# Latent-only projections of the second layer as plain fp32 matmuls on unsplit weights

## The chip, the cores and the metric

The kernel runs on one core of a Trainium2 chip. The metric is the device time of one execution in microseconds, the median of several. Engines: PE (TensorE matmul, with PEld its weight loads), DVE (VectorE), ACT (ScalarE), POOL (GpSimd), SP (SyncE, which issues most DMAs).

## The reference

A two-layer hybrid backbone over 256 latent tokens of width 1024, with 256 context tokens as a prefix. Each layer modulates the tokens, projects them with one combined input matrix, runs four mixers (bidirectional RWKV-7, bidirectional Hyena, short gated convolution, grouped-query attention), merges their outputs through gates, projects, normalises, and runs a mixture of experts.

```python
for l in range(DEPTH):
    ctx_out = l < DEPTH - 1
    h = modulate(x, sh_a, sc_a)
    hc = modulate(ctx, sh_ac, sc_ac)
    pa, pb, pcv, pd, pg = jnp.split(h @ wl, splits, axis=-1)
    ...
    else:                                       # the second layer
        pa_c = hc @ wl[:, :OFF_HYENA]
        pd_c_kv = hc @ wl[:, OFF_ATTN + Q_W:OFF_GATE]
    ya_c, ya = rwkv_mixer(pa_c, pa, ...)
    yd_c, yd = attention_mixer(pd_c_kv, pd_c_q, pd, ...)
    yb = hyena_mixer(pb, ...)
    ycv = short_conv_mixer(pcv, sconv_w[l])
    y = merge_branches((ya, yb, ycv, yd), pg, w_branch[l], w_out[l])
    x = layer_norm(ALPHA * x + g_a * y, ln1_g[l], ln1_b[l])

def merge_branches(ys, gate_proj, w_branch, w_out):
    gates = jax.nn.sigmoid(gate_proj)...
    merged = gates[:, :, 0] * (ys[0] @ w_branch[0])
    for n in range(1, N_BRANCHES):
        merged = merged + gates[:, :, n] * (ys[n] @ w_branch[n])
    return merged @ w_out
```

In the second layer only the latents have an output, so the context enters there through the recurrence and through the attention's keys and values alone. The RWKV receptance (r) and its output gate (g), the attention queries, the Hyena branch, the short convolution and the merge gates read only the 256 latents.

## The kernel before

Tokens lie along the free axis: a layer's modulated input hT has 512 columns, 256 of context and then 256 of latents, and its 1024 channels are eight slices (k) of 128 partitions. Products that need full fp32 are made of three fp32r matmuls: each operand is split into a high part (an ACT copy that rounds, L326) and a low part (a DVE subtraction, L327), and `mm3` (L355 to L357) multiplies high by high, low by high and high by low into one accumulator. The input hT is kept split in tiles hA (high) and hB (low).

`proj` (L716) makes one block of 128 output channels. It takes a weight tile of 128x1024 out of the load ring (`win` and `load`, L711 and L367; one DMA of 1 MB on SP's queue brings two blocks' weights), splits it into one of two tiles cv (`wsplit`), and issues 8 `mm3` into an accumulator. A block takes 512 columns in layer 0 and where the context is needed, and 256 (n0 = 256) for the latent-only blocks of layer 1. The ring has two slots, named "ring".

Layer 1 runs `build_hT1` (transposes, layer norm, modulation), the attention's projections, `rwkv`, whose projections are r, k, v and the low-rank parts, then `hyena` and `sconv` through `block` (six blocks each), `recur` and `merge`. The recurrence is four pairs (`rwkv_pair`): each prepares its decays (PE L876, DVE L877 first), forms products, and inverts a triangular system; the loop L968 and L970 and the passes L990 to L1008 are that inverse, L1012 copies its result. `finish` (L816) normalises and gates the recurrence's output (L841, L844). `merge` (L1288) takes the branches in the order 2, 3, 1, 0. For each of 8 channel blocks it makes one gate block with `proj`, a tanh on ACT (L1323), the branch product (two `mm3` on a split w_branch and a split branch output) and one or two DVE operations (L1330 to L1333). Steps of the adaptive modulation's weight product (`ada_steps`, L394) are put between blocks by `pump`.

Each engine executes its own instructions in a fixed order that the scheduler writes at build time. It sets the order by readiness in its own model, by the source order, and by the buffers: a tile tag such as "R4" or "ring" can be given again only when its last reader is done. Gate blocks are ready early, so the scheduler uses them as fill between the small products of the recurrence.

Of the kernel before, what the change touches and what calls it, by code (L numbers as in the profile page):

```python
# [165 lines left out]
def backbone(ctx: ExitStack, tc: tile.TileContext, a: dict, out: bass.AP, dbg=None):  # L166
# [482 lines left out]
    def build_hT1(arrive, second, third, ups):  # L649

        A = [unit("R9"), unit("TZ")]
        XT = [unit(t).rearrange("p (k c) -> p k c", c=512) for t in ("R4", "R8")]
        hh, hl = big("hA"), big("hB")
# [13 lines left out]
        def modulate(tp, k2):  # L667
            ts_ = slice(tp * 256, tp * 256 + 256)
            q = (ops if k2 % 2 else rps)()
            for j in range(2):  # L670
                for i in range(2):
                    PE.transpose(q[:, (2 * j + i) * 128:(2 * j + i) * 128 + 128],
                                 lnx[2 * tp + i][:, (2 * k2 + j) * 128:(2 * k2 + j) * 128 + 128], ident)
            for j in range(2):
                k = 2 * k2 + j
                src = q[:, j * 256:j * 256 + 256]
                x, h, lo = XT[k // 4][:, k % 4, ts_], hh[k // 4][:, k % 4, ts_], hl[k // 4][:, k % 4, ts_]
                c1, c0 = m[:, tp, 1, k:k + 1], m[:, tp, 0, k:k + 1]
                go(ACT, lambda: ACT.activation(h, src, AF.Identity, scale=c1, bias=c0))
                if k2 % 2:  # L680
                    go(DVE, lambda: DVE.tensor_scalar(x, src, c1, c0, op0=OP.mult, op1=OP.add))
                else:
                    go(ACT, lambda: ACT.activation(x, src, AF.Identity, scale=c1, bias=c0))
                eng = POOL if j else DVE
                go(eng, lambda: eng.tensor_tensor(lo, x, h.bitcast(F32), op=OP.subtract))
# [21 lines left out]
        for k2 in range(4):  # L707
            modulate(1, k2)
        return hh, hl

# [5 lines left out]
    def proj(src, hT, n0, cuts=()):  # L716

        hi, lo = early.pop(0) if early else wsplit(src)
        o = acc()[:, :512 - n0]
        for c0, c1 in zip((n0,) + cuts, cuts + (512,)):  # L720
            for k in range(8):
                mm3(o[:, c0 - n0:c1 - n0], (hi[:, k, :], lo[:, k, :]),
                    (hT[0][k // 4][:, k % 4, c0:c1], hT[1][k // 4][:, k % 4, c0:c1]), k == 0, k == 7)
        return o
# [31 lines left out]
    def rwkv(l, hT, ctx_out):  # L756
# [29 lines left out]
        w = win(l, 2)  # L786
        vTu = unit("R4")
        for b in range(2):
            t = vTu[:, b * 512:b * 512 + 512]
            mix(t, proj(w[:, :, 128 * b:128 * b + 128], hT, 0), l, 4 + b)  # L790
            q = rps()
# [24 lines left out]
        def finish():  # L816

            lb = unit("R4")[:, :256]
            POOL.dma_start(lb, rows_ap(a["rwkv_lnx_b"], l * 256, [[0, 128], [1, 256]]))
# [33 lines left out]
    def rwkv_pair(l, s, b, emit, kTb, rTb, V, Y, wad, wa, bon, N8):  # L853
# [4 lines left out]
        rot[0] += 1  # L858
        F = Cut(unit("R4"))
        kkr, kkd, at, lw = F(256), F(256), F(256), F(256)  # L860
# [329 lines left out]
    def attention(l, hT, ctx_out):  # L1190
        n0 = 0 if ctx_out else 256
        A, B = Cut(unit("R5")), Cut(unit("R6"))
        kt, qs = A(512), [A(512), A(512)]
# [94 lines left out]
    def merge(l, hT, n0, ys, order, finish):  # L1288
        W_ = 512 - n0
        if n0:  # L1290
            m0, WB = unit("R5"), unit("R6", F32R)
            mg = [m0[:, db * W_:db * W_ + W_] for db in range(8)]
        else:
            ms, WB = (unit("R5"), unit("R6")), unit("R8", F32R)
            mg = [ms[db // 4][:, (db % 4) * 512:(db % 4) * 512 + 512] for db in range(8)]
        for oi, n in enumerate(order):
            if oi == FIN[l]:
                ys[0] = finish()
            if oi == 3:
                rg["tags"], rg["n"] = ("ring", "ring", "R2", "R3"), 0  # L1300
                cvr["tags"], cvr["n"] = ("cv0", "cv1", "R4"), 0
            if oi == 3:
                mh, ml = [[unit(t, F32R).rearrange("p (k c) -> p k c", c=512) for t in ts]
                          for ts in (("R0", "R1"), ("R9", "TZ"))]
            pr = unit("R7", F32R)
            yh = pr[:, :1024].rearrange("p (b t) -> p b t", b=2)
            yl = pr[:, 1024:].rearrange("p (b t) -> p b t", b=2)
            split(ys[n][:, :, :W_], yh[:, :, :W_], yl[:, :, :W_])
            if oi == 0:
                raw = wt("y2", [128, 1024])  # L1310
            for db in range(8):
# [3 lines left out]
                if db % 2 == 0:  # L1315
                    wb = raw[:, db % 4 * 256:db % 4 * 256 + 512].rearrange("p (k c) -> p k c", k=2)
                    SP.dma_start(wb, rows_ap(a["w_branch"], (l * 4 + n) * C * D + db * 128,
                                             [[D, 128], [128 * D, 2], [1, 256]]))
                    wbs = WB[:, db % 4 * 512:db % 4 * 512 + 1024].rearrange("p (x k c) -> p x k c", x=2, k=2)
                    split(wb, wbs[:, 0], wbs[:, 1])  # L1320
                gp = proj(wg[:, :, (db % 2) * 128:(db % 2) * 128 + 128], hT, n0)
# [3 lines left out]
                cs = slice((db % 2) * 128, (db % 2) * 128 + 128)  # L1325
                for k in range(2):
                    mm3(q, (wbs[:, 0, k, cs], wbs[:, 1, k, cs]),
                        (yh[:, k, :W_], yl[:, k, :W_]), k == 0, k == 1)
# [407 lines left out]
    for l in range(DEPTH):  # L1736
# [44 lines left out]
        def block(i, wc=wc, l=l, hT=hT, n0=n0):  # L1781
# [3 lines left out]
            return proj(wc[i // 2][:, :, (i % 2) * 128:(i % 2) * 128 + 128], hT, n0)  # L1785

        ys[1] = hyena(l, block, n0, kf)
        ys[2] = sconv(l, lambda j: block(6 + j), n0)
# [165 lines left out]
```

## Time and profile before

| quantity | value |
|---|---|
| median of 3 runs | 1911.12 us (1905.01 to 1916.12) |
| profiled execution, device time | 1914.72 us |
| its span in the trace | 1912.9 us |
| mean granted clock, share of full | 0.934 |
| PE busy | 1679.5 us, 88% of the span |
| DVE busy | 884.5 us, 46% |
| ACT busy | 530.6 us, 28% |

Times of the trace below count from the start of the span. Layer 1's mixers lie from about 1100 to 1634 us. An instruction's duration on PE is that of a pipelined instruction, so the distance from start to start in an undisturbed row is its price, not the duration in its row. "Idle" time in a row stands with the instruction that came before its engine could go on, and PEclk is the granted clock as a share of full.

### The profile page before, as it was taken

How to read it: one execution, taken by the hardware profiler on the slowest of the kernel's cores; microseconds unless marked ns; L12 is line 12 of the kernel's file. 1: busy time of each engine (PE TensorE's matmuls, PEld its weight loads, DVE VectorE, ACT ScalarE, POOL GpSimd, SP SyncE). 2: the span in 40 equal slices, each digit the busy share in tenths (PEclk: the TensorE clock that was granted, in tenths of full speed). 3: DMA queues.
4: the chain of work that ended last, by engine and by line, in shares of the span. 5: the costliest groups of instructions: out<-in, count | busy, mean ns of one | idle time of the engine just before them, and what ended most of it. 6: DMA issues, size and time to landing. Idle time of an engine off the chain costs nothing. (4 is left out here: it accounts for less than half of the span.)

```text
span 1912.9 us, 24847 instructions
## 1 busy us (share of the span) xinstructions
PE 1679.5 (88%) x9683; PEld 1109.7 (58%) x9683; DVE 884.5 (46%) x1920; ACT 530.6 (28%) x935; POOL 223.4 (12%) x263
## 2 busy tenths in 40 slices
PE   4799999999999987999999919989889996999982
PEld 1467666766778875444444306767778895444430
DVE  4364458778554565101010076585887676200003
ACT  2253233433223311111011044543443352111101
POOL 4200121011000031000000041021120002000001
PEclk7899999999999995999999959988899997999996
DMA  9513553111243255883979953265212357879994
GB/s 367 212 40 131 183 188 111 50 62 51 76 138 116 101 196 191 287 337 117 378 273 375 403 196 129 82 224 192 67 62 86 117 180 289 337 281 420 420 421 163
DMA packets 123350, 384.82 MB, mean 201 GB/s; under 512 B 8791, under 2 KB 75103, under 8 KB 92383
## 3 DMA queue, kind: packets, MB, share of 16 engines
q1 hardware_dynamic: 106176, 329.41, 46.0%
q10 hardware_dynamic: 10238, 33.23, 4.7%
q0 software_dynamic: 6816, 20.58, 3.0%
q8 instruction: 77, 1.26, 0.3%
q14 instruction: 43, 0.34, 0.1%
HBM read 361.62 MB, written 21.56 MB: 200 GB/s over the span
## 5 line engine op out<-in xcount | busy, mean ns | idle before, releaser
L357 PE MATMUL acc<-hB,cv 128*128 128x512 f32 (+1 forms) x864 | 309.4, 359 | 9.9 <-POOL hB L616 9.8
L355 PE MATMUL acc<-hA,cv 128*128 128x512 f32 (+1 forms) x864 | 309.2, 358 | 7.1 <-ACT hA L610 3.9
L356 PE MATMUL acc<-hA,cv 128*128 128x512 f32 (+1 forms) x864 | 308.1, 357 | 4.2 <-DVE cv L327 4.2
L355 PEld LDWEIGHTS acc<-hA,cv 128*128 128x128 f32 x864 | 166.2, 192 | 44.6 <-issue 10.1
L357 PEld LDWEIGHTS acc<-hB,cv 128*128 128x128 f32 x864 | 165.8, 192 | 44.5 <-issue 12.8
L356 PEld LDWEIGHTS acc<-hA,cv 128*128 128x128 f32 x864 | 166.1, 192 | 34.4 <-issue 8.4
L327 DVE TENSOR_TENSOR cv<-ring,cv 128x1024 fp32r<-128x1024 f32 (+1 forms) x108 | 128.6, 1197 | 41.9 <-ACT cv L326 39.6
L1415 DVE TENSOR_TENSOR y<-XS,k 128x512 f32<-128x512 f32 x15 | 15.4, 1029 | 266.4 <-PE k L1403 265.7
L326 ACT ACTIVATE cv<-ring 128x1024 fp32r<-128x1024 f32 (+1 forms) x108 | 109.1, 1019 | 27.7 <-DMA ring<-in_w_in_dram 22.4
L1403 PE MATMUL k<-R,R 128*64 128x512 f32 (+1 forms) x288 | 108.5, 600 | 2.9 <-DMA R<-in_exp_w_dram 2.9
L394 PE MATMUL ada<-ring,csf 128*32 128x512 f32 x336 | 63.4, 665 | 13.3 <-ACT csf L230 10.1
L1403 PEld LDWEIGHTS k<-R,R 128*64 128x64 f32 (+1 forms) x288 | 36.6, 152 | 56.5 <-issue 50.8
L1323 ACT ACTIVATE gt<-acc 128x512 f32<-128x512 f32 (+1 forms) x64 | 31.3, 488 | 110.9 <-PE acc L357 102.7
L1403 PE MATMUL acc<-R,R 128*64 128x512 f32 (+1 forms) x160 | 60.3, 594 | 1.7 <-DMA R<-in_exp_w_dram 1.7
L1415 DVE TENSOR_TENSOR y<-XS,acc 128x512 f32<-128x512 f32 x7 | 7.2, 1028 | 114.4 <-PE acc L1403 114.4
L1332 DVE SCALAR_TENSOR_TENSOR gt<-gt,o 128x512 f32<-128x512 f32 (+1 forms) x48 | 26.5, 552 | 69.6 <-PE o L357 66.1
L1403 PE MATMUL k<-ring,R 128*64 128x512 f32 (+1 forms) x144 | 54.4, 609 | 0.0
L968 DVE TENSOR_TENSOR R<-R 128x32 f32<-128x32 f32 (+14 forms) x120 | 50.9, 424 | 1.7
L1535 DVE CAST m_ix<-o 128x1 int32<-128x1 f32 x14 | 2.2, 159 | 106.2 <-PE o L1533 106.2
L355 PE MATMUL o<-R,R 128*128 128x512 f32 (+1 forms) x128 | 45.7, 358 | 2.9 <-DVE R L1330 2.9
L357 PE MATMUL o<-R,R 128*128 128x512 f32 (+1 forms) x128 | 45.6, 358 | 1.1 <-DVE R L327 1.1
L1435 PE MATMUL k<-R,y 128*64 128x512 f32 (+1 forms) x124 | 45.6, 593 | 0.8 <-DVE y L1420 0.8
(565 smaller groups left out, 3386.7 us busy)
## 6 DMA issues: line engine op xcount, KB each, us to landing
R<-in_exp_w_dram SPq DMA_DIRECT2D x87, 1024.0 KB
ring<-in_w_in_dram SPq DMA_DIRECT2D x51, 1024.0 KB
ring<-in_ada_w_dram SPq DMA_DIRECT2D x42, 1024.0 KB
ring<-in_exp_w_dram SPq DMA_DIRECT2D x34, 1024.0 KB
cv<-in_exp_w_dram SPq DMA_DIRECT2D x31, 1024.0 KB
hB<-in_exp_w_dram SPq DMA_DIRECT2D x24, 1024.0 KB
TZ<-in_exp_w_dram SPq DMA_DIRECT2D x16, 1024.0 KB
y<-in_w_branch_dram SPq DMA_DIRECT2D x32, 256.0 KB
```

The source lines that it names most:

```text
L326: first = ACT.activation(hi, src, AF.Copy)
L327: DVE.tensor_tensor(lo, src, hi.bitcast(F32), op=OP.subtract)
L355: PE.matmul(o, lh, rh, start=start, stop=False)
L356: PE.matmul(o, ll, rh, start=False, stop=False)
L357: PE.matmul(o, lh, rl, start=False, stop=stop)
L394: PE.matmul(po[32 * q:32 * q + 32, :], csf[:, 2 * k:2 * k + 32], t[:, 512 * q:512 * q + 512], start=(k == 0), stop=(k == 7), skip_group_ch ...
L968: DVE.tensor_tensor(P4[:, :, :, :i + 1], T4[:, :, :, :i + 1], row[:, None, :, :].to_broadcast([128, 8, 2, i + 1]), op=OP.mult)
L1323: ACT.activation(gt, gp, AF.Tanh, scale=0.5)
L1332: DVE.scalar_tensor_tensor(gt, gt, 1.0, q, op0=OP.add, op1=OP.mult)
L1403: PE.matmul(q[c, :], t[:, k, c], w[x](k), start=(k == 0), stop=(k == 7), skip_group_check=n > 1)
L1415: DVE.tensor_tensor(t.rearrange("p (k c) -> p c k", k=4), act.rearrange("p (c k) -> p c k", k=4), p3.rearrange("p (c k) -> p c k", k=4), o ...
L1435: PE.matmul(p[h][c, :], t[:, k, c], w2[x](k)[:, h * 512:h * 512 + 512], start=(k == 0), stop=(k == 3), skip_group_check=n > 1)
```

## The change

In layer 1 alone, the blocks that read only latents are made of plain fp32 matmuls: `proj` issues 8 matmuls of 128x256 on the fp32 weights as they lie in the load tile and on the fp32 latents, without a split of the weights and without cv tiles. These are 47 blocks: g (1), r (2), Hyena (6), short convolution (6), gates (32). The two blocks of the attention queries, whose weight tile is given as 4-d, keep the split; so do the blocks of 512 columns, layer 0 and the output projection. For this `build_hT1` keeps the modulated latents in fp32 (one tile XT[1], in R4) and hands them out as hT[2]. The branch products of layer 1's `merge` become two plain matmuls per block; their weights are loaded into R7 and neither they nor the branch outputs are split.

R4 is taken by the latents now, so four users of it or of its successors move in layer 1: the v tile to R8, the tiles of `finish` and of the pairs to R6, the attention's second tile to TZ. The ring has more slots in layer 1: after the RWKV projections "ring", "ring", "cv0", "cv1", and two more for the last branch. The accumulator is taken ahead of the split in all blocks.

```diff
     def build_hT1(arrive, second, third, ups):
         A = [unit("R9"), unit("TZ")]
-        XT = [unit(t).rearrange("p (k c) -> p k c", c=512) for t in ("R4", "R8")]
+        XT = [unit(t).rearrange("p (k c) -> p k c", c=256) for t in ("R8", "R4")]
...
-                x, h, lo = XT[k // 4][:, k % 4, ts_], hh[k // 4][:, k % 4, ts_], hl[k // 4][:, k % 4, ts_]
+                x, h, lo = XT[tp][:, k, :], hh[k // 4][:, k % 4, ts_], hl[k // 4][:, k % 4, ts_]
...
-        return hh, hl
+        return hh, hl, XT[1]
...
     def proj(src, hT, n0, cuts=()):
+        o = acc()[:, :512 - n0]
+        if n0 and len(hT) == 3 and len(src.shape) == 3:
+            for k in range(8):
+                PE.matmul(o, src[:, k], hT[2][:, k, :], start=(k == 0), stop=(k == 7))
+            return o
         hi, lo = early.pop(0) if early else wsplit(src)
-        o = acc()[:, :512 - n0]
...
-        vTu = unit("R4")
+        vTu = unit("R8" if l else "R4")
...
-            lb = unit("R4")[:, :256]
+            lb = unit("R6" if l else "R4")[:, :256]
...
-        F = Cut(unit("R4"))
+        F = Cut(unit("R6" if l else "R4"))
...
-        A, B = Cut(unit("R5")), Cut(unit("R6"))
+        A, B = Cut(unit("R5")), Cut(unit("TZ" if l else "R6"))
...
     def merge(l, hT, n0, ys, order, finish):
         if n0:
-            m0, WB = unit("R5"), unit("R6", F32R)
+            m0, raw = unit("R5"), unit("R7")
...
-                rg["tags"], rg["n"] = ("ring", "ring", "R2", "R3"), 0
+                rg["tags"], rg["n"] = ("ring", "ring", "R2", "R3") + (("cv0", "cv1") if n0 else ()), 0
...
-            split(ys[n][:, :, :W_], yh[:, :, :W_], yl[:, :, :W_])
+            if not n0:
...
+                split(ys[n][:, :, :W_], yh[:, :, :W_], yl[:, :, :W_])
...
-                    split(wb, wbs[:, 0], wbs[:, 1])
+                    if not n0:
...
+                        split(wb, wbs[:, 0], wbs[:, 1])
...
                 for k in range(2):
+                    if n0:
+                        PE.matmul(q, wb[:, k, cs], ys[n][:, k, :W_], start=(k == 0), stop=(k == 1))
+                        continue
                     mm3(q, (wbs[:, 0, k, cs], wbs[:, 1, k, cs]),
                         (yh[:, k, :W_], yl[:, k, :W_]), k == 0, k == 1)
...
+        if l:
+            rg["tags"], rg["n"] = ("ring", "ring", "cv0", "cv1"), 0
         ys[1] = hyena(l, block, n0, kf)
         ys[2] = sconv(l, lambda j: block(6 + j), n0)
         recur()
```

The order on the engines moves with it. Line numbers of the changed kernel are 4 higher from `rwkv` on (L876 is L880 there) and 9 or 10 higher in the end of `merge`. The first rows are PE's before, at the first recurrence pair of layer 1. Names: acc is a block's accumulator, cv a split weight tile, k a small accumulator of the recurrence, ada that of the modulation.

```order
L355 MATMUL acc_7866<-hA_1140_6964,cv_1275_7863 128x256
L356 MATMUL acc_7866<-hA_1140_6964,cv_1275_7863 128x256
L357 MATMUL acc_7866<-hB_1142_6966,cv_1275_7863 128x256
L876 MATMUL k_8340<-R_1324_8337,cst 64x256 x2
L883 MATMUL k_8346<-R_1243_7538 128x256
L884 MATMUL k_8347<-R_1243_7538 128x256
L883 MATMUL k_8371<-R_1243_7538 128x256
L884 MATMUL k_8372<-R_1243_7538 128x256
L355 MATMUL acc_7922<-hA_1139_6963,cv_1281_7919 128x256
L355 MATMUL acc_7953<-hA_1139_6963,cv_1283_7950 128x256
L394 MATMUL ada_7199<-ring_7896,csf 32x512 x4
```

The same place on PE in the changed kernel, where R_1138 is the tile of fp32 latents and L721 the new matmul:

```order
L394 MATMUL ada_7852<-cv_1297_7969,csf 32x512 x4
L721 MATMUL acc_7985<-R_1138_6962,ring_7961 128x256 x2
L721 MATMUL acc_8021<-R_1138_6962,cv_1301_7996 128x256 x8
L394 MATMUL ada_7852<-ring_7998,csf 32x512 x4
L721 MATMUL acc_8035<-R_1138_6962,cv_1301_7996 128x256 x5
L394 MATMUL ada_7852<-ring_8004,csf 32x512 x4
L721 MATMUL acc_8035<-R_1138_6962,cv_1301_7996 128x256 x3
L880 MATMUL k_8055<-R_1309_8052,cst 64x256 x2
L887 MATMUL k_8061<-R_1243_7538 128x256
L888 MATMUL k_8062<-R_1243_7538 128x256
L887 MATMUL k_8086<-R_1243_7538 128x256
L888 MATMUL k_8087<-R_1243_7538 128x256
```

Before, acc_7866 is the second of the six Hyena blocks; the other four and the short convolution's six stand behind the recurrence's first products (acc_7922 and acc_7953 are the next two). In the changed kernel all twelve stand ahead of them, acc_8035 being the last.

The second place is DVE in the inverse loop of a recurrence pair, before (L1046, L1072 and L1077 are the other pair's work):

```order
L970 TENSOR_REDUCE R_1427_9038<-R_1427_9038 128x16
L1077 TENSOR_SCALAR Sf_9160<-sbd_92,ssc_8487 128x128
L968 TENSOR_TENSOR R_1427_9038<-R_1427_9038 128x16x5
L327 TENSOR_TENSOR cv_1617_10152<-ring_10109,cv_1617_10152 128x1024
L970 TENSOR_REDUCE R_1427_9038<-R_1427_9038 128x16
L1072 COPY Wn_9131<-k_9128 128x128
L968 TENSOR_TENSOR R_1427_9038<-R_1427_9038 128x16x6
L1046 COPY_PREDICATED am_86<-msk,k_9138 128x128
```

and in the changed kernel, in the same loop:

```order
L972 TENSOR_TENSOR R_1412_8753<-R_1412_8753 128x16x5
L1341 SCALAR_TENSOR_TENSOR gt_9808<-gt_9808,o_9810 128x256
L974 TENSOR_REDUCE R_1412_8753<-R_1412_8753 128x16
L1342 TENSOR_TENSOR R_1566_9575<-R_1566_9575,gt_9808 128x256
L972 TENSOR_TENSOR R_1412_8753<-R_1412_8753 128x16x6
L1076 COPY Wn_8846<-k_8843 128x128
L974 TENSOR_REDUCE R_1412_8753<-R_1412_8753 128x16
```

The split of the weights is gone from between the links of the loop. What still stands there is the gate arithmetic of `merge` and the other pair's work.

## Rows read from the trace of the kernel before

**Rows 1.** The page: busy time, share of the span and instructions of each engine.

```profile
PE 1679.5 (88%) x9683; PEld 1109.7 (58%) x9683; DVE 884.5 (46%) x1920; ACT 530.6 (28%) x935; POOL 223.4 (12%) x263
```

**Rows 2.** Timeline (start, length), and L1012 by its line, in layer 1.

```profile
1241.75 0.60 PE L793 MATMUL k<-cst,R 128*128 128x128 f32 x4
...
1248.57 0.41 DVE L877 TENSOR_SCALAR R<-k 128x256 f32<-128x256 f32 x1
...
L1012 DVE COPY TZ<-TZ x8: 269/288/291, 1331.3 to 1480.5; 64x256 f32<-64x256 f32 x8
...
1512.98 0.41 PE L844 MATMUL k<-cst,R 128*128 128x128 f32 x2 [1.05 <-DVE R L841]
```

**Rows 3.** Windows from first pair to finish, and tail; columns first.

```profile
core 0: us, PE busy (x) PEld busy (x) DVE busy (x) ACT busy (x) POOL busy (x), PEclk, DMA share, GB/s
1248.60:1331.30 82.70, 72.94 (x591) 53.34 (x587) 60.01 (x129) 34.58 (x65) 17.88 (x23) 0.88 0.59 202
1331.30:1383.90 52.60, 46.82 (x472) 40.50 (x470) 41.46 (x107) 23.19 (x47) 9.03 (x9) 0.90 0.26 85
1383.90:1435.40 51.50, 45.87 (x480) 39.52 (x475) 44.41 (x110) 24.41 (x50) 11.05 (x10) 0.93 0.20 66
1435.40:1480.20 44.80, 43.34 (x485) 38.68 (x485) 35.50 (x88) 16.71 (x31) 2.44 (x2) 1.00 0.27 86
1480.20:1512.40 32.20, 31.67 (x264) 29.16 (x260) 17.77 (x56) 10.27 (x22) 1.76 (x3) 1.00 0.14 43
sum 263.80, PE 240.64 PEld 201.20 DVE 199.14 ACT 109.16 POOL 42.16; mean PE 48.13 PEld 40.24 DVE 39.83 ACT 21.83 POOL 8.43
...
1513.00:1570.00 57.00, 54.98 (x451) 54.22 (x452) 42.48 (x75) 28.00 (x47) 0.38 (x1) 0.97 0.58 190
```

**Rows 4.** The same windows, DVE's splits of L327 alone (us, busy, count).

```profile
1248.60:1331.30 82.70, 14.67 (x12) 0.88 0.59 202
1331.30:1383.90 52.60, 8.29 (x9) 0.90 0.26 85
1383.90:1435.40 51.50, 8.71 (x8) 0.93 0.20 66
1435.40:1480.20 44.80, 6.24 (x6) 1.00 0.27 86
1480.20:1512.40 32.20, 3.13 (x3) 1.00 0.14 43
```

**Rows 5.** PE's waits from 1100 to 1600: us in total, times, longest.

```profile
PE acc L356 <- DVE cv L327: 4.2, 3, 2.8
...
PE acc L355 <- ACT cv L326: 2.2, 5, 0.8
```

**Rows 6.** Timeline of DVE in the inverse loop.

```profile
1397.86 0.30 DVE L968 TENSOR_TENSOR R<-R 128x80 f32<-128x80 f32 x1
1398.08 1.22 DVE L327 TENSOR_TENSOR cv<-ring,cv 128x1024 fp32r<-128x1024 f32 x1
1399.21 0.23 DVE L970 TENSOR_REDUCE R<-R 128x16 f32<-128x80 f32 x1
```

**Rows 7.** Timeline of PE at the end of the gates and the output projection.

```profile
1568.89 0.28 PE L357 MATMUL acc<-hB,cv 128*128 128x256 f32 x1
...
1569.95 0.28 PE L357 MATMUL acc<-hB,cv 128*128 128x256 f32 x1
...
1570.75 0.39 PE L355 MATMUL acc<-R,R 128*128 128x512 f32 x1
```

**Rows 8.** Plain fp32 matmuls, and a modulation step: timeline and one line's records.

```profile
227.03 3.19 PE L1157 MATMUL o<-cst,R 128*128 128x256 f32 x14
230.06 3.18 PE L1145 MATMUL o<-R,cst 128*128 128x256 f32 x14
...
1291.23 1.07 PE L394 MATMUL ada<-ring,csf 128*32 128x512 f32 x8
...
L1157 PE MATMUL o<-cst,R x48: 377/379/483, 224.6 to 1290.9; 128*128 128x256 f32 x48
```

## What I predict, before the changed kernel has run

> **What bounds the kernel now.** I read the page first: PE is busy for 88% of the span and DVE for 46% [rows 1]. That is a mean over stages, and the change touches only layer 1's mixers, so I cut that stretch by what ends its stages. The four passes of the recurrence end where the copies of L1012 and then the finish at L844 run [rows 2]. In a table by stage [rows 3] PE is busy for 240.6 of the 263.8 us from the first recurrence pair to the finish, and DVE for 199.1. Both are needed: the passes are a chain of small PE products and small DVE operations, and the gate blocks are fill between them. Where PE runs out of fill the granted clock falls (0.88 in the first stage, 0.90 and 0.93 in the next two, 1.00 later). The tail from the finish to the output projection is PE alone: 54.98 of 57 us. The splits stand in the DVE column of a second table [rows 4]: 41.0 us of L327 in the five stages. The waits show hardly any of that on PE: 4.2 and 2.2 us [rows 5]. They cost on DVE's own chain instead: a split of 1.22 us stands between two links of the inverse loop, L968 and L970, on an engine that runs in a written order [rows 6].
>
> **The price of a block.** The old block issues three fp32r matmuls of 128x256 per k-slice. In an undisturbed row of them the starts are (1569.95 - 1568.89) / 9 = 0.118 us apart [rows 7], so 0.353 us per k-slice. The new one issues one plain fp32 matmul on the same 256 columns. The trace before has such matmuls in the hyena transforms: L1157 and L1145, both with fp32 operands. The program issues L1157 24 times and the trace has 48 records, so each is two records; 14 records take 230.06 - 227.03 = 3.03 us [rows 8], 0.216 each, so 0.433 us per matmul. The change therefore adds 0.08 us of PE per k-slice. It makes 47 blocks of 8 and 32 branch products of 2, 440 matmuls: 440 x 0.433 = 190.5 against 1320 x 0.118 = 155.8, **+34.7 us of PE work**. Removed are 47 block splits, 1.2 us of DVE each [rows 6], the branch splits, and the ACT copy that goes ahead of each.
>
> **Where it lands, by the order of the changed program.** Up to the second transposes of V (L793, at 1241.75 [rows 2]) 85 fp32r matmuls (10.0 us) become 28 plain ones (12.1): +2.1. The relaid latents put some of the filter's DVE work ahead of the last step of the input transposition: 0 to 3 us, I take 0.4. V's second transposes then come at 1244.3.
>
> The largest step is one that the diff doesn't name. Before, PE's first recurrence product stands shortly behind V's transposes, and most hyena and short-convolution blocks are fill beside the first pass; DVE's L877 ran at 1248.57 [rows 2]. Now PE has all the hyena and short-convolution blocks ahead of it: 92 plain matmuls x 0.433 = 39.8; ten steps of the modulation of 1.07 us each [rows 8] = 10.7; the transforms, 16 plain matmuls = 6.9 and 0.5 of small ones. That is 57.9 us. I add 3.6 for waits: the transforms wait for POOL and ACT in a chain, and the weight tiles are now read straight from the load ring, so a slot is free only after its last matmul; the loads behind it in SP's queue wait, and so does PE. The loads there are 16 tiles of 1.05 MB in 61.5 us, 273 GB/s. The first stage moved 202 GB/s at a share of 0.59 [rows 3], which scales to 342, so 80%: I bound the ring at 0 to 6 us. First pair: 1244.3 + 61.5 = **1305.8 and a little, 1306, 57.5 us later** than before.
>
> In return the first pass runs without all that. Between L877 and the inverse DVE now has 95 instructions. Without its splits it had 60.0 - 14.7 = 45.3 us for 117 before, 0.39 each, so 37 us busy [rows 3, 4]. Idle time on top: at least the 14 us that DVE had in the last short stage (32.2 - 17.8), at most the 22.7 of the first one. 51 to 60 us; I take 56, nearer to the first stage, whose chain and low clock this is. That is 26.7 us less than 82.7. **First inverse: +31 us.**
>
> Passes two to finish took 181.1 us. On DVE 8.3 + 8.7 + 6.2 + 3.1 = 26.4 us of splits go [rows 4]; if all of it comes back, 155 us. PE's fill there hardly changes its price: 495 fp32r matmuls (58.4 us) make way for 134 plain ones (58.0), since part of the gates now stands ahead of the first inverse. So PE's own busy time, 167.7 us [rows 3], is the other bound, less some 4.5 us if the clock were full through the stretch; from there to the 176 that would be if only splits beside an idle PE came back. I take 167: **-14 us.** What is late next is PE's chain of small products, not the splits.
>
> The tail: 126 plain matmuls x 0.433 = 54.6 us and about 0.7 at its start, against 57.7 (1512.98 to 1570.75) [rows 2, 7]: -2.4. The first matmuls after it wait less for branch splits: -1.
>
> Edits at nothing: the moved buffers (R4 to R8 or R6, R6 to TZ), since no row shows a wait for these tags in layer 1; the earlier call of the accumulator; everything in layer 0, the output projection and the experts, whose instructions stand in the old order.
>
> **Sum.** 31 - 14 - 2.4 - 1 = +13.6, against the profiled execution of 1914.7 us: 1928.3. The median of the runs shown, 1911.1, is 0.2% below that execution, so on its terms 1924.7, **1925 us**. Bounds by the terms: first stage -5 to +4, the later passes -12 to +9, the ring -2 to +4, the filter -0.4 to +2.6; not all at once, so the forecast's own range is 1911 to 1939.
>
> **Rivals.**
>
> Rival A, the other side: PE takes the extra work into its gaps. From the first pair to the finish it idles 23.2 us, and at the clocks of the table some 9.9 + 5.3 + 3.6 = 18.8 us are lost to the lower level; with DVE freed of 41 us of splits PE could run through both. Then 263.8 - 42.0 + 34.7 = 256.5, -7.3, and with the tail -10.7: 1904, or 1900 on the median's terms. For it: the splits stand inside the inverse loop. Against it: the gaps lie where the chain waits, and the new order takes the fill away from the first pass, where 9.8 us of them and most of the lost clock are. It decides if PE idles under 8 us from the first pair to the finish, at a clock of 0.98 or more. The Trainium skill, "Perfetto Trace Analysis", section Identifying the Most-Contended Engine, says that busy matmul time is a poor measure of TensorE's headroom and that the weight loads' busy share should be read too. By that rule 201.2 of 263.8 us, 76%, leave 62.6 us in which all the new work is hidden, and the time would be near rival A's. I trust the matmul starts, which the rows show back to back at 0.118 us.
>
> Rival B: nothing comes back. The splits may have been hidden beside PE's 92%; the passes two to finish keep their 181 us, and +31 - 3.4 gives 1942, or 1939. With the ring's upper bound, 1943. For it: the few us that PE visibly waits for splits [rows 5]. Against it: DVE waits little too in passes two and three, 41.5 and 44.4 us busy of about 52.
>
> Rival C: the plain matmul is cheaper than the transforms make it look, 0.216 us, because one of the two records is the profiler's. Then the change doesn't add but removes PE work; 92 and 126 matmuls lie on the path, 218 x 0.216 = 47 us less than the forecast: 1881, or 1878. Against it: 14 records really occupy 3.03 us of the timeline, with the next engine's work behind them. The Trainium skill, "Perfetto Trace Analysis", section Engine Utilization, halves the array's rate for fp32 in a footnote, which would be about that price; the trace doesn't agree, at 0.433 us for 256 columns.
>
> **How the numbers follow.** Forecast 0.62, A 0.15, B 0.20, C 0.03. One half per cent, 9.6 us, is about what a measurement of this kernel can tell from no change. Faster by more: half of A and all of C, 0.11. Within: the other half of A and the lower third of the forecast's range, 0.27. Slower: 0.62. The range takes in most of A and B: 1903 to 1941 leaves out part of A, C and the top of B, some 0.2.
>
> **What would show it.** The new blocks' matmul starts: 0.43 us per matmul (right), 0.22 (C). The first L881 (before's L877) at about 1306 on the trace's axis; if it is before 1290, the order isn't kept by the chip's waits as I read it. First inverse near 1362; finish near 1529, 163 to 172 us after it: 181 speaks for B, under 158 for A. Output projection near 1585. The granted clock of the first pass at 0.9 or less. I am wrong if the gap between the inverse and the finish doesn't shrink by at least 8 us, or if the stretch ahead of the first pair takes under 50 us.

## The result, and the profile after

The changed kernel takes 1926.1 us (median of 9 runs, 1921.1 to 1931.0) against 1916.0 for the kernel before (9 runs). The ratio is 1.0056, 95% interval 1.0033 to 1.0080: slower, by some 11 us. A ratio of 1 lies outside the interval. The interval's middle is above the half per cent that the prediction takes as the least a measurement can tell, its lower end below. The profiled execution has a span of 1924.1 us against 1912.9.

The two traces have to be compared by stretch. Layer 0's order is unchanged, yet its last inverse stands at 496.9 us before and 492.8 after, and in twelve other kernels with the same layer 0 between 490.5 and 500.5; behind the router (the first product of the experts' gate, at 1603.5 and 1609.5) the traces of all kernels take 308 to 315 us. So one trace says nothing about 5 us there. What is compared below is the stretch from V's second transposes to the router: 361.8 us before, 372.0 after, +10.2.

The stage table of the changed kernel, to be held against [rows 3], with columns in the first row. The stages are: V to the first pair, the first pass, three passes, the last pass up to the finish, the tail, the output projection up to the router.

```profile
core 0: us, PE busy (x) PEld busy (x) DVE busy (x) ACT busy (x) POOL busy (x), PEclk, DMA share, GB/s
1237.50:1299.90 62.40, 62.20 (x319) 43.13 (x317) 13.61 (x27) 5.75 (x13) 7.17 (x12) 1.00 0.78 281
1299.90:1348.00 48.10, 41.45 (x342) 32.46 (x342) 36.22 (x95) 20.51 (x47) 9.34 (x13) 0.93 0.34 106
1348.00:1391.80 43.80, 40.53 (x401) 31.31 (x395) 35.91 (x100) 17.01 (x39) 7.59 (x9) 1.00 0.19 61
1391.80:1440.60 48.80, 45.50 (x410) 35.04 (x410) 36.03 (x101) 17.93 (x41) 8.02 (x9) 0.97 0.17 55
1440.60:1486.60 46.00, 44.66 (x445) 35.96 (x441) 30.01 (x83) 11.45 (x24) 4.47 (x3) 1.00 0.31 96
1486.60:1520.60 34.00, 32.39 (x222) 26.94 (x219) 15.82 (x53) 4.93 (x14) 3.10 (x4) 1.00 0.03 10
1520.60:1577.30 56.70, 55.67 (x258) 48.42 (x258) 20.27 (x47) 14.59 (x29) 0.31 (x1) 1.00 0.50 172
1577.30:1609.50 32.20, 24.60 (x104) 19.34 (x104) 20.62 (x29) 7.32 (x9) 8.30 (x6) 0.94 0.85 324
sum 372.00, PE 347.01 PEld 272.59 DVE 208.50 ACT 99.49 POOL 48.30; mean PE 43.38 PEld 34.07 DVE 26.06 ACT 12.44 POOL 6.04
```

The same stretch before, the stages that [rows 3] lacks, and the sum over all eight:

```profile
1241.70:1248.60 6.90, 6.90 (x57) 5.24 (x55) 2.31 (x5) 2.24 (x5) 0.00 (x0) 1.00 0.98 338
...
1480.20:1513.00 32.80, 31.69 (x265) 29.21 (x261) 18.20 (x57) 10.56 (x22) 2.36 (x3) 1.00 0.14 43
1513.00:1570.75 57.75, 55.73 (x457) 54.97 (x458) 43.23 (x75) 28.75 (x48) 0.38 (x1) 0.97 0.58 188
1570.75:1603.50 32.75, 24.42 (x106) 19.24 (x104) 21.23 (x30) 9.48 (x12) 7.18 (x6) 0.95 0.91 342
sum 361.80, PE 327.72 PEld 280.70 DVE 266.33 ACT 149.93 POOL 50.32; mean PE 40.96 PEld 35.09 DVE 33.29 ACT 18.74 POOL 6.29
```

PE's busy time grew by 19.3 us, and its idle time fell from 34.1 to 25.0. Busy time at half clock counts double, so I take it out: each stage's length times (1 - PEclk), summed, is 22.4 us before and 6.6 after, with the last two stages taken as one, as for every kernel below (22.2 and 6.8 by the rows as shown; the clock has two digits). What is left, **PE's work at the full clock, is 305.3 us before and 340.4 after: +35.1**, and the time **lost to idle and half clock fell from 56.5 to 31.6: -24.9**. The difference of the two is the result. By the prediction's price the 412 plain matmuls of this stretch (28 of the 440 stand ahead of it) add 32.6 us; the measure gives 2.5 us more, and between kernels with the same PE work, before and no_split in the table below, it scatters by 3. The splits of [rows 4] have no counterpart in the passes any more. Four lines of PE's timeline show the new order and the new price:

```profile
1297.76 1.56 PE L721 MATMUL acc<-R,cv 128*128 128x256 f32 x6
1299.25 0.65 PE L880 MATMUL k<-R,cst 64*64 64x256 f32 x4
...
1563.67 3.62 PE L721 MATMUL acc<-R,R 128*128 128x256 f32 x16
1567.12 1.03 PE L1334 MATMUL o<-y,R 128*128 128x256 f32 x4
```

Sixteen records (8 matmuls) take 1567.12 - 1563.67 = 3.45 us, 0.431 each. The first recurrence product comes at 1299.25, behind the last block of the short convolution.

### The profile page after: what moved, and what is told of

It is laid out like the page before. It is cut to its first block, busy times and chain, and to the rows that moved or that the text cites. A ratio compares the mean times of both kernels' runs of the same rounds, so it can differ in the third digit from the quotient of the medians.

```text
span 1924.1 us, 23810 instructions
## 1 busy us (share of the span) xinstructions
PE 1704.8 (89%) x9243; PEld 1107.7 (58%) x9243; DVE 821.9 (43%) x1853; ACT 476.2 (25%) x868; POOL 222.9 (12%) x263
## 5 line engine op out<-in xcount | busy, mean ns | idle before, releaser
L357 PE MATMUL acc<-hB,cv 128*128 128x512 f32 (+1 forms) x504 | 203.0, 403 | 7.6 <-POOL hB L616 7.6
L355 PE MATMUL acc<-hA,cv 128*128 128x512 f32 (+1 forms) x504 | 203.9, 405 | 4.9 <-ACT hA L610 3.9
L356 PE MATMUL acc<-hA,cv 128*128 128x512 f32 (+1 forms) x504 | 201.7, 401 | 0.0
L355 PEld LDWEIGHTS acc<-hA,cv 128*128 128x128 f32 x504 | 96.2, 191 | 39.1 <-issue 10.5
L357 PEld LDWEIGHTS acc<-hB,cv 128*128 128x128 f32 x504 | 95.9, 190 | 34.7 <-POOL hB L616 9.4
L356 PEld LDWEIGHTS acc<-hA,cv 128*128 128x128 f32 x504 | 96.1, 191 | 21.6 <-issue 3.2
L721 PE MATMUL acc<-R,ring 128*128 128x256 f32 x400 | 99.8, 390 | 0.0
L327 DVE TENSOR_TENSOR cv<-ring,cv 128x1024 fp32r<-128x1024 f32 (+1 forms) x66 | 76.2, 1158 | 23.2 <-ACT cv L326 23.0
L721 PEld LDWEIGHTS acc<-R,ring 128*128 128x128 f32 x400 | 73.2, 192 | 13.8 <-issue 4.1
L721 PE MATMUL acc<-R,cv 128*128 128x256 f32 x288 | 74.0, 390 | 0.0
L326 ACT ACTIVATE cv<-ring 128x1024 fp32r<-128x1024 f32 (+1 forms) x66 | 65.3, 1000 | 21.2 <-DMA ring<-in_w_in_dram 12.0
L1412 PEld LDWEIGHTS k<-R,R 128*64 128x64 f32 (+1 forms) x288 | 36.5, 151 | 56.5 <-issue 50.6
L721 PEld LDWEIGHTS acc<-R,cv 128*128 128x128 f32 x288 | 51.0, 190 | 12.3 <-issue 5.2
```

The costliest lines, as they stand in the source:

```text
L326: first = ACT.activation(hi, src, AF.Copy)
L327: DVE.tensor_tensor(lo, src, hi.bitcast(F32), op=OP.subtract)
L355: PE.matmul(o, lh, rh, start=start, stop=False)
L356: PE.matmul(o, ll, rh, start=False, stop=False)
L357: PE.matmul(o, lh, rl, start=False, stop=stop)
L721: PE.matmul(o, src[:, k], hT[2][:, k, :], start=(k == 0), stop=(k == 7))
```

## Experiments

PE's work, idle time and clock loss are worked out for each kernel as above, from V's second transposes to the router. Each kernel has one trace, and the change that it shows can differ from that of the ratio by up to 6 us (pool_early: +20.0 us in the trace, +14.0 by the ratio), so a few us between two traces decide nothing.

| kernel | ratio to before, 95% interval | PE work | idle | lost to clock | V to router, us |
|---|---|---|---|---|---|
| before | 1 | 305.3 | 34.1 | 22.4 | 361.8 |
| changed kernel | 1.0056 (1.0033 to 1.0080) | 340.4 | 25.0 | 6.6 | 372.0 |
| gates_only | 1.0013 (0.9998 to 1.0028) | 332.5 | 25.2 | 9.9 | 367.7 |
| blocks_only | 1.0039 (1.0020 to 1.0059) | 313.3 | 38.9 | 18.5 | 370.8 |
| recur_first | 1.0062 (1.0046 to 1.0079) | 341.8 | 26.4 | 7.9 | 376.1 |
| old_recur_first | 0.9990 (0.9973 to 1.0007) | 305.8 | 33.6 | 19.2 | 358.6 |
| ring2 | 1.0029 (1.0007 to 1.0051) | 339.5 | 25.8 | 4.4 | 369.7 |
| dummy_split | 1.0104 (1.0064 to 1.0143) | 339.6 | 29.6 | 10.7 | 379.9 |
| one_low | 0.9944 (0.9922 to 0.9966) | 306.1 | 28.1 | 15.7 | 349.9 |
| no_split | 0.9948 (0.9924 to 0.9972) | 308.2 | 30.1 | 17.5 | 355.8 |
| pool_early | 1.0073 (1.0045 to 1.0101) | 306.0 | 45.9 | 29.9 | 381.8 |
| early_gates | 0.9977 (0.9958 to 0.9997) | 322.6 | 26.0 | 7.6 | 356.1 |
| early_gates_rf | 1.0020 (0.9998 to 1.0042) | 323.4 | 30.4 | 16.7 | 370.5 |
| early_gates2 | 0.9961 (0.9945 to 0.9978) | 318.2 | 25.2 | 10.8 | 354.2 |

### Which half of the change costs, and which gives back

```diff
 gates_only (from the changed kernel)
-        if n0 and len(hT) == 3 and len(src.shape) == 3:
+        if n0 and plain:                   # plain=True is passed by merge alone
...                                        # the four ring slots come only behind recur()
 blocks_only (from the changed kernel)
+        # merge as before: gates and branch products split; F and lb in R4
```

> Only the 32 gate blocks and the 32 branch products of layer 1 are plain fp32; g, r, Hyena and short-convolution blocks keep the split, and the ring takes the cv tiles only after them. Its PE order has the first recurrence pair behind two Hyena blocks, as the kernel before has. Theory (price plus order): the first pair comes at about 1248 us as before, the passes from the first inverse to the finish shorten from 181 to 164-168 us, because 26 us of DVE splits are gone, and the tail holds 186 plain steps of 0.433 us, 80 us instead of 58. Sum +6 to +10 us against the kernel before (ratio 1.003 to 1.005). Rival (PE price alone): 320 steps of 0.08 us, +25 us, ratio 1.013.

> The other half: g, r, Hyena and short-convolution blocks (15) are plain fp32, gates and branch products keep the split. Its PE order has all Hyena and short-convolution blocks ahead of the first recurrence pair, as the changed kernel has. Theory: the first pair comes at about 1300 us, the first pass takes 50-56 us, the passes to the finish stay near 181 us because the gate splits are still on DVE, and the tail shrinks to about 33 us. Sum 0 to +5 us (ratio 1.000 to 1.003). Rival (PE price alone): 15 blocks of 0.62 us, +9 us. Rival (the late first pair is the whole cost): +10 us or more, and gates_only no slower than before.

gates_only costs +2.5 us by its ratio, less than the +6 to +10 expected, with an interval that includes no change; blocks_only +7.5, more than the 0 to +5, and what the rival "PE price alone" gave (+9). By the ratios they add up to the whole (10.0 of 10.7 us); the traces overshoot it (5.9 + 9.0 against 10.2). In PE's work both are near the step price: +27 for 320 steps (25 by the price), +8 for the 96 steps of the blocks behind V. The loss falls by 21 us with the gates and not at all with the blocks (57.4 against 56.5). These two runs alone don't refute the rival "the late first pair is the whole cost", since gates_only, with an early pair, is not clearly slower than before; recur_first does. The three passes and the finish of gates_only are those that the prediction took for the changed kernel, 166.2 us at a granted clock of 1.00:

```profile
1324.20:1368.20 44.00, 40.70 (x399) 31.10 (x395) 35.43 (x98) 16.73 (x38) 7.75 (x9) 1.00 0.21 66
1368.20:1411.60 43.40, 40.82 (x402) 31.41 (x398) 36.06 (x100) 17.82 (x41) 7.59 (x9) 1.00 0.20 62
1411.60:1457.40 45.80, 44.46 (x442) 35.91 (x438) 28.91 (x78) 11.35 (x24) 2.42 (x2) 1.00 0.27 85
1457.40:1490.40 33.00, 32.02 (x222) 26.59 (x217) 15.32 (x53) 4.92 (x14) 2.33 (x3) 1.00 0.13 42
```

### Does the late first pair cost anything

```diff
 recur_first (from the changed kernel); old_recur_first (from the kernel before)
+        if l:
+            recur()
         ys[1] = hyena(l, block, n0, kf)
         ys[2] = sconv(l, lambda j: block(6 + j), n0)
-        recur()
+        if not l:
+            recur()
 ring2 (from the changed kernel): the ring of before
-                rg["tags"], rg["n"] = ("ring", "ring", "R2", "R3") + (("cv0", "cv1") if n0 else ()), 0
+                rg["tags"], rg["n"] = ("ring", "ring", "R2", "R3"), 0
...
-        if l:
-            rg["tags"], rg["n"] = ("ring", "ring", "cv0", "cv1"), 0
```

> The changed kernel with one edit: in layer 1 the recurrence stands ahead of Hyena and the short convolution in the source, so that they are fill beside it. All plain matmuls stay. The first pair stands right behind V's transposes again. Theory: PE's total work stays; what can be won is PE's idle time and half-clock time between V and the finish (15.8 and 4.8 us in the changed kernel), at most half of it: -8 to +2 us against the changed kernel, so 0 to +12 against before. Rival (the order is the whole cost): as fast as the kernel before or faster, -10 us or more against the changed kernel.

> The kernel before with the same edit (recurrence ahead of Hyena and short convolution in layer 1). Theory: the first pair was early already and PE is 91% busy from there to the finish, so within 5 us of before. Rival (source order matters by itself): faster by 8 us or more here too, so that a gain of recur_first would not belong to the plain matmuls.

> The changed kernel with the load ring of before (two slots, and R2 and R3 for the last branch). With it the PE order has the first recurrence pair behind two Hyena blocks again, as before, with all plain matmuls kept: so the four slots, not the plain matmuls, moved it. Theory: the first pair at about 1245 us, the first pass 75-85 us, and the stretch from V to the router as in the changed kernel, 370-378 us, since PE's work is the same: 1.004 to 1.008 of before. Rival (the late first pair is a cost of its own): 8 us or more faster than the changed kernel. Rival (four slots are needed for the plain matmuls' loads): slower than the changed kernel by more than 5 us.

Nothing that these runs can tell. With the pair at 1241.6 us (recur_first), at 1253.1 (ring2) and at 1299.9 (the changed kernel) PE's work is 340 to 342 us and the loss 30 to 34. recur_first, at 1.0062, is no faster than the changed kernel; ring2, at 1.0029, has an interval that overlaps the changed kernel's and leaves room for a few us. old_recur_first stays within its 5 us of before (0.9990). Fill that stands ahead of the recurrence is missing from the tail, and the other way round: recur_first's tail takes 104.1 us, the changed kernel's 56.7. ring2 also shows what had moved the pair: the ring of four slots ahead of the Hyena blocks, one line of the diff, and not the plain matmuls. (dummy_split, below, keeps that line and drops the longer ring of the last branch, and its pair stays late, at 1308.4.) The longer ring bought nothing measurable here.

### What gives time back: DVE's splits, or the plain blocks as fill

```diff
 dummy_split (from the changed kernel; two ring slots for the gates)
+                if n0:
+                    wsplit(wg[:, :, (db % 2) * 128:(db % 2) * 128 + 128])     # result unused
...
 one_low (from the kernel before)
...
+                    ACT.activation(hp_, ws, AF.Copy)
+                    if not one:
+                        one.append(DVE.tensor_tensor(lp_, ws, hp_.bitcast(F32), op=OP.subtract))
 no_split (from one_low): the high part, the branch outputs' and w_branch's parts also only once
```

> The changed kernel with the old split of the gate weights put back beside the plain matmuls, unused (ACT copy and DVE subtraction into the cv tiles, 32 times; two ring slots for the gates). PE's work is that of the changed kernel. Theory: the loss on PE between V and the router returns from 31.8 us towards 56, so 12 to 24 us slower than the changed kernel, 1.011 to 1.018 of before. Rival (splits are hidden beside PE): within 5 us of the changed kernel, 1.003 to 1.008 of before.

> The kernel before, with its three fp32r matmuls everywhere, but layer 1's gate blocks all use one low part of the weights, computed once, so that 31 DVE subtractions of 1.2 us fall away while the ACT copies and PE's work stay (a part of the computation is left out here: the low parts belong to the first gate block). From V's transposes to the router the kernel before takes 361.8 us: 305.6 of PE work at the full clock and 56.2 lost to idle and half clock. Theory (the subtractions stand in DVE's chain and open the gaps on PE): the loss falls to 33-40 us, 339-346 us for the stretch, 16 to 22 us faster than before, passes of about 160 us. Rival (the subtractions are hidden; the gaps came back in the changed kernel because PE has other fill): within 5 us of before.

> The kernel before with three fp32r matmuls everywhere, and layer 1's gate blocks and branch products all on the parts of the first gate block and the first branch, so that no ACT copy and no DVE subtraction is left for them (the values of the later blocks are left out; loads and PE's work stay). From V to the router PE's work is again about 306 us. one_low, without the gates' subtractions alone, lost 43.8 us there to idle and half clock, gates_only 35.2, before 56.5. Theory A (all of the loss that came back is the splits on ACT and DVE): 31 to 37 us lost, the stretch at 337-343 us, 19 to 25 us faster than before, ratio 0.987 to 0.990. Theory B (a third to half came back because plain blocks give PE more fill per block, not because engines were freed): 41 to 45 us lost, like one_low, ratio 0.993 to 0.996.

Both, in shares that the runs bound only roughly. one_low and no_split leave out a part of the computation: the low parts, in no_split the high parts too, are right for the first blocks alone. Put back beside the plain matmuls, the gates' splits (ACT's copies included) raise the loss from 31.6 to 40.3 (+8.7). By the ratios dummy_split is 9 us slower than the changed kernel, less than the 12 to 24 expected, and with four runs its interval overlaps the changed kernel's. Without DVE's subtractions the old matmuls lose 43.8 instead of 56.5 (-12.7; one_low is 11 us faster than before, less than the 16 to 22 expected). But without any split for the gates and the branch products (no_split) they lose 47.6, no less than one_low. That is above what either theory gave, 31 to 37 if the splits were everything and 41 to 45 if a third to half came with the plain blocks. So some 9 to 13 of the 24.9 us that came back go with the gates' splits, and the rest, by subtraction, comes with the plain matmuls themselves. The passes show in what form. The sum over the three passes and the finish of no_split:

```profile
sum 180.80, PE 168.57 PEld 147.11 DVE 121.47 ACT 55.24 POOL 22.82; mean PE 42.14 PEld 36.78 DVE 30.37 ACT 13.81 POOL 5.71
```

of one_low:

```profile
sum 177.50, PE 166.16 PEld 146.10 DVE 121.54 ACT 74.66 POOL 23.53; mean PE 41.54 PEld 36.53 DVE 30.39 ACT 18.66 POOL 5.88
```

and of dummy_split:

```profile
sum 179.00, PE 168.07 PEld 133.92 DVE 134.24 ACT 65.16 POOL 24.26; mean PE 42.02 PEld 33.48 DVE 33.56 ACT 16.29 POOL 6.07
```

no_split's DVE is busy for 121.5 us, gates_only's for 115.7, and yet its passes take 180.8 us against 166.2. Of the 14.6 us between them 2 are PE's work, 4 idle time (12.2 against 8.2) and 8.5 the clock, which falls after waits at which PE has no fill. Most of these waits stand in or just ahead of the inverse's products. PE in slices of 3 us (length, busy, granted clock, DMA), in the kernel before:

```profile
1361.00:1364.00 3.00, 3.00 (x27) 1.00 0.02 5
1364.00:1367.00 3.00, 0.61 (x7) 1.00 0.00 0
1367.00:1370.00 3.00, 2.08 (x32) 0.69 0.00 0
1370.00:1373.00 3.00, 1.62 (x5) 0.50 0.01 3
1373.00:1376.00 3.00, 3.00 (x31) 0.50 0.28 93
1376.00:1379.00 3.00, 3.00 (x63) 0.61 0.00 0
```

in no_split:

```profile
1417.00:1420.00 3.00, 0.47 (x5) 0.95 0.00 0
1420.00:1423.00 3.00, 3.00 (x35) 0.50 0.00 0
1423.00:1426.00 3.00, 3.00 (x38) 0.50 0.01 3
1426.00:1429.00 3.00, 2.96 (x58) 0.91 0.00 0
```

and in gates_only, at the same place of its second pass:

```profile
1354.00:1357.00 3.00, 1.63 (x8) 1.00 0.00 0
1357.00:1360.00 3.00, 2.92 (x62) 1.00 0.02 5
```

The wait that ends the gap, from the timeline of the kernel before:

```profile
1366.87 0.30 PE L990 MATMUL k<-TZ,y 64*64 64x64 f32 x2 [2.39 <-DVE TZ L982]
```

of no_split:

```profile
1419.86 1.12 PE L990 MATMUL k<-TZ,y 64*64 64x64 f32 x16 [2.53 <-DVE TZ L1003]
```

and of gates_only:

```profile
1357.08 1.15 PE L994 MATMUL k<-TZ,y 64*64 64x64 f32 x32 [1.45 <-POOL R L961]
```

In the kernel before the fill ahead of the inverse's products runs out 2.4 us before DVE and ACT have transposed the loop's result (L981, L982). The clock falls to the lower of its two levels, and PE, the inverse's chain of products included, runs at half speed for about 10 us (by the clocks of the slices, 6 x (0.31 + 0.50 + 0.50 + 0.39)). In no_split the wait of the shown spell is for the masked copy L1003 between two steps of the inverse; another of its spells follows a wait of 2.46 us outside the inverse, of L1070 for ACT's L1066. In gates_only, at the place that corresponds to that of the kernel before, PE waits 1.45 us, by the profile for a POOL operation that follows the transposes, and keeps the full clock. Summed over the passes the clock costs 8.9 us before (52.6 x 0.10 + 51.5 x 0.07), 8.5 in no_split, 5.1 in one_low, 1.5 in dummy_split and the changed kernel, 0 in gates_only. Why the gap is shorter with plain blocks isn't settled: the scheduler chose the fill anew in each kernel, and no run here holds the order and changes the price alone.

```diff
 pool_early (from the kernel before)
-                gp = proj(wg[:, :, ...], hT, n0)
+                gp = proj(wg[:, :, ...], hT, n0, eng=POOL if n0 and oi < 2 else None)
```

> The kernel before, complete, with one edit: in layer 1 the low parts of the gate weights of the first two branches are subtracted on POOL instead of DVE (16 times; POOL is busy for 50 of 362 us there, and takes 2.35 us for a subtraction of this size elsewhere in this kernel). PE keeps the fp32r price. Theory (the subtraction costs where it stands in DVE's chain): the loss on PE falls from 56.5 towards one_low's 43.8, so 5 to 12 us faster than before, 0.994 to 0.997, faster than early_gates if the upper half holds. Rival (POOL's own steps of the recurrence are delayed by 2.4 us pieces as DVE's were by 1.2): within 5 us of before or slower.

The expected gain of 5 to 12 us did not come. The rival holds, and more: 14 us slower than before, passes of 202.3 us. POOL's subtraction takes 2.50 us, and some of DVE's operations wait for its end (last section); how the 14 us divide between the two was not tested.

### A version that is faster than both

```diff
 early_gates (from gates_only)
-                gp = proj(wg[:, :, ...], hT, n0, plain=True)
+                gp = proj(wg[:, :, ...], hT, n0, plain=oi < 2)
...                                        # the ring of before for the last two branches
 early_gates_rf: the edit of recur_first on it
 early_gates2 (from early_gates): branch products of the last two branches split again
-                    if n0:
+                    if pl:                 # pl = n0 and oi < 2
                         PE.matmul(q, wb[:, k, cs], ys[n][:, k, :W_], start=(k == 0), stop=(k == 1))
```

> Plain fp32 only for the gates of the first two branches, which are fill beside the recurrence, and for the branch products; the gates of the last two branches, most of which run when PE is alone, keep the split, as do g, r, Hyena and the short convolution. Against gates_only 128 steps go back from 0.433 to 0.353 us, 10.2 us of PE in a stretch where DVE has been idle for two thirds of the time. Theory: 7 to 11 us less than gates_only, 0.996 to 1.000 of before. Rival (the splits cost as much in the tail as in the passes): like gates_only or slower, 1.001 or more.

> early_gates with the recurrence ahead of Hyena and the short convolution in the source (as old_recur_first, 3.2 us less from V to the router than before). Its PE order has fp32r blocks as fill for the first three passes and plain gates only from the fourth on. Theory: the plain steps then stand partly in the tail where they give nothing back, and the splits of the Hyena blocks stand beside the passes: 357 to 364 us from V to the router, 0.998 to 1.003 of before, slower than early_gates. Rival (the order helps by itself): 353 us or less, below early_gates.

> early_gates with the branch products of the last two branches back on the split too, so that plain fp32 is left only where it is fill beside the recurrence. Another 32 steps go back from 0.433 to 0.353 us, 2.6 us of PE in the tail. PE's work from V to the router is then about 320 us against 305.3 before and 322.6 in early_gates. Theory (PE's work plus a loss of 32 to 36 us once the fill of the passes is plain): 351 to 356 us for the stretch, ratio to before 0.995 to 0.998, passes of 166 us at a granted clock of 1.00 as in early_gates. Rival (the split branch outputs are awaited in the tail): as early_gates or slower, 0.998 or more.

early_gates keeps the gain of the passes (166.3 us) and has 128 plain steps fewer than gates_only. It is 0.23% faster than before, and early_gates2 0.39% (0.9945 to 0.9978), 18 us below the changed kernel; both came as expected. early_gates_rf came out within its ratio but missed its stretch (370.5 us, not 357 to 364): with fp32r Hyena blocks as the fill of the passes the clock loss is back, 16.7 us, and the plain steps stand in the tail. The passes and the tail of early_gates2:

```profile
1329.50:1372.80 43.30, 40.76 (x400) 31.09 (x395) 34.30 (x97) 16.62 (x38) 7.99 (x9) 1.00 0.22 67
1372.80:1416.20 43.40, 40.77 (x398) 31.41 (x398) 36.05 (x99) 17.83 (x41) 7.58 (x9) 1.00 0.20 62
...
1495.10:1564.50 69.40, 68.92 (x542) 67.02 (x543) 49.33 (x85) 35.25 (x59) 3.07 (x2) 1.00 0.50 168
```

The tail has the splits back on DVE (49.3 of 69.4 us) and PE doesn't wait for them (68.92 of 69.40 busy).

## Why the prediction was right, and where its steps were not

The time was right: 1925 us predicted, 1926 measured, within the forecast's own range and on the side that it gave 0.62. That it came within 1 us is luck: the forecast added 13.6 us to a kernel whose three runs had a median of 1911.1, while nine runs of it have 1916.0 and the change measured 10.7. Step by step:

- **The price of a block** held: 0.433 us taken from L1157, 0.431 in the new blocks; 32.6 of the 34.7 us of PE work lie in the stretch, which shows +35.1. Rival C falls. The Trainium skill, Perfetto Trace Analysis, section Engine Utilization, halves the array's rate for what it calls FP32_LOW_HIGH. One record of a plain matmul, at 0.216 us beside 0.118 for an fp32r matmul of the same size, comes near that; the whole matmul, which is two records, doesn't.
- **Up to V** was mis-sized: +2.5 us, measured -0.1 (744.8 us from layer 0's last inverse before, 744.7 after), within what one trace scatters.
- **The late first pair** held to a microsecond: 61.7 us from V to it, measured 62.4, but in another division: 57.9 of work and 3.6 of waits were taken, PE was busy for 62.20. The ring, bounded at 0 to 6 us, shows no gap there. 1306 on the axis became 1299.9 because V stood 6.8 us earlier than forecast, 4.1 of it already at the end of layer 0's last inverse.
- **The first pass** was 8 us too long: 56 taken, 48.1 measured, at a granted clock of 0.93 where 0.9 or less was forecast. DVE's 37 us busy came as 36.2; the idle time was 12 and not 19, below the row that I had taken as its lower end.
- **The passes to the finish** were 5 us too short: 167 taken against 181.1, measured 172.0 up to the same finish. The sum's 4.5 us for a full clock there is half of what rival A takes from the same two rows (5.3 + 3.6).
- **The tail** gave -1.0 instead of -2.4, the output projection up to the router -0.6 against -1.

The errors of the first pass and of the passes nearly cancel, so part of the closeness is luck. And the reasons were only half right. "The largest step is one that the diff doesn't name" turned out to be no cost: moving the first pair by 50 us changed nothing that could be measured (recur_first, ring2), and the line that moved it stood in the diff. What I read as a cost of 57 us and returns of 27 and 14 was PE's work in another order. The return is not "26.4 us of splits go" either: a third to a half of it goes with the gates' splits, the rest is gaps and clock that changed with the fill, which the prediction named (less 4.5 us if the clock were full) but only for passes that it thought bound by PE's chain. Rival B's reason (the splits are hidden) falls with one_low; rival A's (PE takes the work into its gaps) was right in mechanism, since 24.9 us of 56.5 came back, but not in size: PE idled for 16.2 us from the first pair to the finish (23.2 before) at 0.93 to 1.00, where it asked for 8 us and 0.98. The room that the weight loads leave (62.6 us) was not there: PE's work grew in full, and only 24.9 us of idle time and clock paid for it.

## What to carry to other kernels

Where one engine is busy for nine tenths of a stretch and its instructions can be moved freely, cost a change as that engine's work at the full clock plus what it loses to idle and half clock; moving work about in the stretch then cancels, and only the loss is worth arguing over. Order still counts where it changes the loss: early_gates_rf loses 47.1 us where early_gates loses 33.5. In this kernel plain fp32 was the better block as fill beside the recurrence's chain, the split one where PE is alone: choose by place, not for the whole layer.

## What the runs showed of the hardware

A subtraction of 128x1024 from two SBUF operands takes 1.22 us on DVE [rows 6] and 2.50 on POOL. While it runs on POOL, a DVE operation that starts after it and reads two SBUF tensors is held until its end: in the ten cases of pool_early between 1340 and 1500 us the DVE operation ends 0.1 to 0.5 us behind POOL's. In pool_early, POOL's splits, as a group:

```profile
L327 POOL TENSOR_TENSOR cv<-ring,cv 128x1024 fp32r<-128x1024 f32 x16 | 39.9, 2498 | 91.6 <-ACT cv L326 85.0 <-PE k L1041 6.7
```

One of them, the DVE multiplication that starts beside it, and the same line where it started ahead of POOL's operation (an L906 at 1433.31):

```profile
1383.13 2.58 POOL L327 TENSOR_TENSOR cv<-ring,cv 128x1024 fp32r<-128x1024 f32 x1
...
1383.37 2.63 DVE L904 TENSOR_TENSOR R<-R 128x256 f32<-128x256 f32 x1
...
1433.27 0.43 DVE L904 TENSOR_TENSOR R<-R 128x256 f32<-128x256 f32 x1
```

The kernel before has the same in small, beside a POOL product of its own:

```profile
1368.81 0.64 POOL L906 TENSOR_TENSOR R<-R,R 128x256 f32<-128x256 f32 x1
1368.88 0.86 DVE L904 TENSOR_TENSOR R<-R 128x256 f32<-128x256 f32 x1
```

L904 ends 0.29 us behind POOL's operation in both (1386.00 against 1385.71, 1369.74 against 1369.45), so 0.86 us is no undisturbed length; 0.43 is. The inverse loop's L968, a product of two tensors, went from 411 to 554 ns in the mean over three passes, its reduction L970 stayed at 296 and 294. The groups of pool_early:

```profile
L968 DVE TENSOR_TENSOR R<-R 128x32 f32<-128x32 f32 (+14 forms) x45 | 24.9, 554 | 0.5
L970 DVE TENSOR_REDUCE R<-R 128x16 f32<-128x32 f32 (+14 forms) x45 | 13.2, 294 | 0.4
```

L968 and L904 read two SBUF tensors, L970 one. An operation with one SBUF input was held too, a copy of L1012 (1.86 us beside a split, 0.29 in the median). The Trainium skill, GPSIMD Engine Reference, section Specifications, says that POOL's SBUF interfaces are shared with VectorE and that DVE instructions with two SBUF inputs contend there; these rows agree. That POOL stood nearly idle in the page of the profile was no sign that work could be moved to it.
